# A two-layer encoder trunk on one core: wide products of a weight piece ahead of its narrow ones, and seven-product couples at the front of each pair

## The chip, the core and the metric

The kernel runs on one core of one Trainium2 chip. The metric is the time of one execution on the device in microseconds (us). The kernel before was timed three times; the median counts. One more execution was profiled, and all rows of the trace come from that one.

## What is computed

The reference takes x (256 tokens by 2048 features, float32) through two layers and a last RMSNorm. Cut to what matters:

```python
for layer in range(2):
    hn = rmsnorm(h, norm_mix_g[layer])
    h = h + (mlstm_mixer(hn, ...) if layer == 0 else hgrn_mixer(hn, ...))
    h = h + conv_glu(rmsnorm(h, norm_ffn_g[layer]), w_up[layer], conv_w, conv_b, w_down[layer])
return rmsnorm(h, final_g)

def conv_glu(hn, w_up, conv_w, conv_b, w_down):
    a, v = split(hn @ w_up, 2)          # 2048 -> 2 x 5504
    c = conv_b + sum of three shifted a * conv_w
    return (gelu(c) * v) @ w_down       # 5504 -> 2048
```

Nearly all the work is products with weights, in float32 accuracy, that are read once.

## The kernel before, in words

**Two-part numbers.** TensorE (PE) is given a rounded format, so each operand is sent as a high part and the rest. ScalarE (ACT, L149) casts a raw weight piece of 1024 columns to `wh`, VectorE (DVE, L150) subtracts to get `wl`. An activation tile `xt` holds 256 high and 256 low columns, one for each token. A product with feature-major output ("fm") is two matmuls with a weight block of 128x128 as the stationary operand: `wh` with all 512 columns of `xt` (L338, the wide one), and `wl` with the 256 high columns alone (L342, the narrow one). A 1024-column piece holds four input tiles by two output blocks, thus eight wide and eight narrow matmuls. Line 329 lists them as wide, narrow, wide, narrow, and so on; the tuple `swap` names places where two neighbours change places.

**Stages.** A list of chunks is walked by `stream`: an mLSTM mixer, its output projection, then the feed-forward part of layer 0, the HGRN2 mixer with its projection, and the feed-forward part of layer 1. A feed-forward part has its 43 blocks of 128 hidden features in two parts of 22 and 21 (`FA`, `FB`). Each part is an up pass of as many fm chunks (four pieces each; its results `g`, a high and low half, stay in SBUF), followed by two down pairs. A pair computes two 512-column stretches of the output for both halves of the tokens. In the trace the up passes stand at 400 to 639, 745 to 987, 1690 to 1922 and 2033 to 2266 us, the pairs behind each.

**Pairs.** In a pair, two hidden blocks (a couple, `u`) make a 2x2 block product. The plain way (L297 on) takes eight products, each of three matmuls (high by high, high by low, low by high) of 512 columns: 24 matmuls. Couples listed in `SEVEN` are done in seven products, 21 matmuls, by sums of operand blocks: of the activations (`sx`, made by `token_sums` on DVE at L558 when the second block of the couple has come out of the up pass) and of the weights (`T`). The weight sums of all listed couples but one are made ahead and written to scratch in DRAM (`tscr`), by accumulating DMAs issued on GpSimd (POOL, L611) or on DVE during the up passes (`prepare`, L630), and loaded with the couple; those of couple `FLY` are made on DVE when it is reached (L203). A stored couple loads 1536 raw columns (L137), 1536 columns of sums (L199) and 512 more (L200); a plain couple loads 2048 raw columns. `raw` has three buffers; the `T` tiles share their three (`avc`, L186) with the epilogue of the up chunks (`done_up`, L1178). Pieces are fetched three ahead of their use (`LOOK`).

Four of the products go to banks `mm` of PSUM, and when the last listed couple is through, `mid` (L578) empties them with one copy on ACT, six adds on DVE and two on POOL, by way of a tile `u` with the tag `jk`. The other sums (`pc`) are added at the end of the pair (`done`, L591). In the second pair of a part that ends a layer the last couples are done bank by bank (`tail`, L246), and `bank` of the next norm takes each bank as it is complete: it adds it to the residual `hm`, squares it on ACT (L534, whose output tile has the tag `jk` too), and transposes it (L422) or, at the end of the program, scales it and sends it out (L499 to L530).

**Order.** A scheduler with a timeline of its own sets each engine's order of instructions; `pin` (`keep_in_program_order`) keeps those it is given in the order of the code. Small work is spread between the products by `side.push`, and `tick` moves its clock on.

Of the kernel before, what the change touches and what calls it, by code (L numbers as in the profile page):

```python
# [8 lines left out]
F32 = mybir.dt.float32  # L9
F32R = mybir.dt.float32r  # L10
I32 = mybir.dt.int32
AF = mybir.ActivationFunctionType
# [3 lines left out]
P = 128  # L16
T = 256
# [29 lines left out]
LEAD = 48  # L47
TEMP = 3
GATES = 4 * AH
SEVEN = (1, 2, 3, 4, 5, 6, 7, 8, 9), (1, 2, 3, 4, 5, 6, 7, 8)  # L50
FLY = 5
STORED = 2 * (len(SEVEN[0]) + len(SEVEN[1]) - 2)
BY_TRANSFERS = (9, 27.0), (17, 33.0)
FIRST = 11, 7
# [12 lines left out]
def trunk_kernel(ctx, tc, xT, x_d, fg_d, pp_d, cst_d, w_gate, w_first, w_aq, w_ak, w_av, w_ao, w_aout, w_ao2,  # L67
                 w_bq, w_bv, w_bg, w_bout, w_bo2, w_up, w_d0, w_d1, out, mscr, tscr):
    nc = tc.nc
    act, dve, pool, pe = nc.scalar, nc.vector, nc.gpsimd, nc.tensor  # L70

    keep = ctx.enter_context(tc.tile_pool(name="keep", bufs=1))
# [21 lines left out]
    class Side:  # L94
        def __init__(self):
            self.now, self.jobs, self.behind = 0.0, [], []
# [26 lines left out]
    side, held = Side(), []  # L123


    class Chunk:
        def __init__(self, kind, src, nk, x, done, before=None, swap=(), first=False, paced=False):
            self.swap, self.first, self.paced = swap, first, paced
            self.kind, self.src, self.nk, self.x, self.done, self.before = kind, src, nk, x, done, before
            self.width = {"fm": 256, "tm": 512, "st": 512}[kind]  # L130

    pin = tc.keep_in_program_order
# [90 lines left out]
    def banks():  # L223
        return [psm.tile([P, 512], F32, tag="mm", name="mm") for _ in range(2)]
# [81 lines left out]
    def stream(chunks):  # L306
        pieces = split_weights(chunks)
        ready = []

        def fetch():  # L310
            p = next(pieces, None)
            if p is not None:
                ready.append(p)

        for _ in range(LOOK):
            fetch()
        for ch in chunks:
            if ch.before:
                ch.before()
            if ch.kind == "st":  # L320
                squares_by_seven(ch, fetch, ready)
                continue
            ps = banks()
            k = 0
            while k < ch.nk:
                fetch()
                wh, wl, n = ready.pop(0)
                if ch.kind == "fm":
                    ops = [(kk, f, part) for kk in range(n) for f in range(2) for part in "hl"]
                    for i in ch.swap:  # L330
                        i -= 2 * k
                        if 0 <= i < 2 * n - 1:
                            ops[2 * i + 1:2 * i + 3] = ops[2 * i + 2], ops[2 * i + 1]
                    for kk, f, part in ops:
                        x = ch.x(k + kk)
                        c = kk * ch.width + f * P
                        if part == "h":
                            pe.matmul(ps[f], wh[:, c:c + P], x, start=k + kk == 0, stop=False)  # L338
                            continue
                        if f:  # L340
                            side.tick(0.65)
                        pe.matmul(ps[f][:, 0:T], wl[:, c:c + P], x[:, 0:T], start=False, stop=k + kk == ch.nk - 1)  # L342
                    k += n
                    continue
                for kk in range(n):
                    x = ch.x(k)
                    st, sp = k == 0, k == ch.nk - 1
                    c = slice(kk * 512, (kk + 1) * 512)
                    ops = [(t, i) for t in range(2) for i in range(3)]
                    if ch.first and st:  # L350
                        ops.sort(key=lambda o: (0, 2, 1)[o[1]])
                    for t, i in ops:
                        a, w = ((0, wh), (0, wl), (T, wh))[i]
                        pe.matmul(ps[t], x[:, a + t * P:a + (t + 1) * P], w[:, c], start=st and i == 0, stop=sp and i == 2)  # L354
                    side.tick(1.3)
                    k += 1
            ch.done(ps)
# [21 lines left out]
    class Norm:  # L379
# [46 lines left out]
        def bank(self, ps, i):  # L426
            h = hm[:, i // 2, 512 * (2 + i % 2):512 * (3 + i % 2)]
            dve.tensor_tensor(h, h, ps, ALU.add)
            if i == 3:
                self.add(3)  # L430
                return
            if i == 2:
                self.squares(2)
            for k0 in ((0, 2), (8, 10), (4, 6))[i]:
                self.two(k0, psm.tile([P, 512], F32, tag="mm", name="mm"), pin)
# [34 lines left out]
    class FinalNorm:  # L470
# [5 lines left out]

        def load(self):
            self.g = [keep.tile([P, 512], F32, tag=f"xt{c}", name=f"fg{c}") for c in range(4)]
            for c in range(4):
                pool.dma_start(self.g[c], fg_d[:, c * 512:(c + 1) * 512].broadcast_to([P, 512]))  # L480

        def add(self, c):
            cs = slice(512 * c, 512 * c + 512)
# [15 lines left out]
        def bank(self, ps, i):  # L499
            if i == 0:  # L500
                side.drain()
            t, c = i // 2, 2 + i % 2
            h, total, rc = hm[:, t, 512 * c:512 * c + 512], self.ss[:, t, c:c + 1], self.rc[:, t:t + 1]
            pin(dve.tensor_tensor(h, h, ps, ALU.add))
            if c == 2:
                square(h, total)
                if t:
                    self.store(0)
                pin(dve.scalar_tensor_tensor(rc, total, 1.0 / D, rc, ALU.mult, ALU.add))
                return  # L510
            last = keep.tile([P, 512], F32, tag=f"xt{4 + t}", name="fl")
            pin(dve.scalar_tensor_tensor(last, h, 1.0, h, ALU.mult, ALU.mult, accum_out=total))
            pin(dve.scalar_tensor_tensor(rc, total, 1.0 / D, rc, ALU.mult, ALU.add))
            pool.tensor_tensor(rc, rc, hmx[:, 0:1], ALU.pow)
            v = hm[:, t, 1024:1536]
            pin(dve.tensor_tensor(v, v, self.g[2], ALU.mult))
            if t:
                self.store(1)
# [13 lines left out]
    def square(src, total, pin=lambda ins: ins):  # L532
        jk = ev.tile([P, 512], F32, tag="jk", bufs=1, name="jk")
        pin(act.activation(jk, src, AF.Square, accum_out=total))  # L534
# [630 lines left out]
    def ffn(layer, norm, nxt):  # L1165
# [4 lines left out]
        def begin():  # L1170
            box["mp"] = stack.enter_context(tc.tile_pool(name="ff", bufs=1))
            box["mp"].tile([P, LEAD], F32, name="lead")
            for ch in pairs:
                ch.pool = box["mp"]
            if isinstance(nxt, FinalNorm):
                nxt.begin(box["mp"])
# [28 lines left out]
        for part, (f0, nf) in enumerate(((0, FA), (FA, FB))):  # L1205
            GT, SX, seven = [], {}, SEVEN[part]

            def prep(part=part, nf=nf):
                if part == 0:
                    begin()  # L1210
                n = BY_TRANSFERS[layer][0]
                jobs = todo[n:n + FIRST[layer]] if part == 0 else todo[n + FIRST[layer]:]
                side.push(prepare(box["mp"], jobs, (nf * 10.4 - 26.0) / len(jobs)), True)

            for i in range(nf):
                chunks.append(Chunk("fm", w_up[layer, f0 + i], KT, norm.x, done_up(f0 + i, i, GT, SX, seven),
                                    prep if i == 0 else None,
                                    swap=((2, 12), (2,))[layer] if part and i == 0 else (3,) if f0 + i == 1 else (), paced=True))

            for c0, src in ((0, w_d0[layer][:, f0 * 1024:(f0 + nf) * 1024]), (2, w_d1[layer][:, f0 * 1024:(f0 + nf) * 1024])):  # L1220
                ch = pair(src, nf, c0, lambda k, GT=GT: GT[k], lambda u, SX=SX: SX[u], nxt if part else None, seven)
                ch.waits = []
                for u in seven:
                    if u != FLY:
                        ch.stored[u] = tscr[box["n"]]
                        ch.waits.append(True)
                        todo.append((src[:, 2048 * u:2048 * (u + 1)], tscr[box["n"]], ch.waits))
                        box["n"] += 1
                pairs.append(ch)
                chunks.append(ch)  # L1230
            if part and isinstance(nxt, FinalNorm):
                pairs[-2].before = nxt.load
                pairs[-1].bank, pairs[-1].order = nxt.bank, range(4)
            elif part:
                pairs[-2].later = True
                pairs[-1].bank, pairs[-1].order = nxt.bank, (0, 2, 1, 3)
# [8 lines left out]
    for i in range(90):  # L1245
        o = i % 4 * QUAD
# [6 lines left out]
    c = hgrn(n2, n3)  # L1253
# [108 lines left out]
```

## Time and profile before

| what | value |
|---|---|
| median of 3 runs | 2386.35 us (2380.95 to 2389.92) |
| the profiled execution: its time, its span | 2386.37 us, 2384.4 us |
| PE, DVE, ACT, POOL busy | 99%, 84%, 58%, 12% of the span |
| mean granted clock of PE | 0.998 |
| DMA | 624.32 MB moved, mean 262 GB/s |

The profiled execution lies within 0.02 us of the median, and 1.97 us of its time lie outside the span. Matmuls are pipelined: one is recorded with some 390 ns though the next starts some 230 ns after it, so starts say more than busy times. The waits of an engine are listed by what ended them; "issue" is time in which the profile names nothing.

### The profile page before, as it was taken

What the parts mean: (1) busy time and instruction counts of PE and PEld (TensorE: products, weight loads), DVE (VectorE), ACT (ScalarE), POOL (GpSimd) and SP (SyncE); (2) the same over time, 40 slices, a digit from 0 to 9 for tenths busy, and PEclk for the clock granted to TensorE, in tenths of its full rate; (3) what the DMA queues carried; (4) which work ended last, traced back from release to release, by engine and by line L of the source; (5) the groups of instructions that cost most, each with busy time, mean ns of one, the idle gap of its engine ahead of it and who ended that gap; (6) DMA issues with size and microseconds to landing.
All of it is one profiled execution on the core that took longest, in us unless ns stands there. A gap on an engine that the chain in (4) does not pass through costs nothing.

```text
span 2384.4 us, 38410 instructions
## 1 busy us (share of the span) xinstructions
PE 2361.6 (99%) x14524; PEld 2019.2 (85%) x14524; DVE 1998.9 (84%) x3254; ACT 1393.0 (58%) x2201; POOL 282.4 (12%) x348
## 2 busy tenths in 40 slices
PE   9999999999999999999999999999999999999997
PEld 7888888888888888888888888888888888888876
DVE  7766677988899888898898989889779889888888
ACT  7655455555565555676555555556556576455565
POOL 0110111000000000001333333331010000000000
PEclk9999999999999999999999999999999999999999
DMA  8766878888798888796777777767897788777785
GB/s 299 215 212 232 257 221 274 309 296 289 275 340 305 292 278 280 272 328 219 223 222 232 211 236 222 221 213 235 279 309 274 245 307 325 265 248 243 246 322 203
DMA packets 122986, 624.32 MB, mean 262 GB/s; under 512 B 13856, under 2 KB 14368, under 8 KB 74672
## 3 DMA queue, kind: packets, MB, share of 16 engines
q1 hardware_dynamic: 106128, 590.59, 70.1%
q0 software_dynamic: 16096, 30.48, 8.3%
q8 instruction: 114, 1.87, 0.3%
q10 hardware_dynamic: 576, 0.79, 0.1%
q14 instruction: 72, 0.59, 0.1%
HBM read 584.00 MB, written 92.34 MB: 284 GB/s over the span
## 4 chain that ended last, share of the span: by engine, by line
PE 85%; DVE 5%; DMA 5%; issue 2%; ACT 1%; POOL 1%; SPq 0%; POOLq 0%; DVEq 0%; ACTq 0%
PE mm L338 33%; PE mm L342 17%; PE mm L354 16%; PE pc L236 9%; PE mm L236 7%; DVE wl L150 3%; DMA raw<-in_w_up 1%; DMA T<-tscr 1%; DMA pwh<-in_w_d 1%; DMA raw<-in_w_d 1%; DMA pwl<-in_w_d 1%; PE pn L845 1%; ACT wh L149 1%; PE py L1102 1%; PE pd L1052 0%
## 5 line engine op out<-in xcount | busy, mean ns | idle before, releaser
L338 PE MATMUL mm<-xt,wh 128*128 128x512 f32 x3776 | 1317.9, 394 | 0.0
L150 DVE TENSOR_TENSOR wl<-raw,wh 128x1024 fp32r<-128x1024 f32 (+1 forms) x844 | 1033.7, 1229 | 242.9 <-ACT wh L149 237.0
L149 ACT CAST wh<-raw 128x1024 fp32r<-128x1024 f32 (+1 forms) x844 | 875.2, 1043 | 564.6 <-PE mm L338 295.7
L342 PE MATMUL mm<-xt,wl 128*128 128x256 f32 x3776 | 1051.6, 280 | 1.8 <-issue 1.2
L338 PEld LDWEIGHTS mm<-xt,wh 128*128 128x128 f32 x3776 | 705.8, 187 | 158.9
L342 PEld LDWEIGHTS mm<-xt,wl 128*128 128x128 f32 x3776 | 711.5, 188 | 7.4 <-issue 2.0
L354 PE MATMUL mm<-wh,xt 128*128 128x512 f32 x1024 | 321.7, 393 | 1.8 <-ACT xt L360 1.6
L236 PE MATMUL pc<-wh,g 128*128 128x512 f32 x696 | 237.8, 390 | 0.0
L354 PEld LDWEIGHTS mm<-wh,xt 128*128 128x128 f32 x1024 | 192.1, 188 | 42.2 <-ACT xt L360 2.1
L354 PE MATMUL mm<-wl,xt 128*128 128x512 f32 x512 | 198.7, 392 | 0.0
L236 PE MATMUL mm<-wh,sx 128*128 128x512 f32 x444 | 157.2, 389 | 0.3 <-ACT wh L149 0.3
L149 ACT CAST wh<-T 128x1024 fp32r<-128x1024 f32 (+1 forms) x148 | 122.2, 835 | 55.9 <-DMA T<-tscr 15.6
L236 PEld LDWEIGHTS pc<-wh,g 128*128 128x128 f32 x696 | 130.6, 188 | 27.2
L150 DVE TENSOR_TENSOR wl<-T,wh 128x1024 fp32r<-128x1024 f32 (+1 forms) x148 | 141.5, 967 | 13.1 <-ACT wh L149 12.8
L588 POOL TENSOR_TENSOR hm<-hm,u 128x512 f32<-128x512 f32 x10 | 14.8, 1478 | 1090.4 <-DVE u L587 813.5
L236 PE MATMUL pc<-wl,g 128*128 128x512 f32 x348 | 135.7, 390 | 0.5 <-DVE wl L150 0.5
L354 PEld LDWEIGHTS mm<-wl,xt 128*128 128x128 f32 x512 | 96.6, 189 | 19.1
L1184 ACT COPY avc<-mm 128x256 f32<-128x256 f32 x172 | 64.1, 372 | 69.4 <-PE mm L342 69.4
L236 PEld LDWEIGHTS mm<-wh,sx 128*128 128x128 f32 x444 | 83.2, 188 | 18.0 <-ACT wh L149 0.8
L236 PE MATMUL mm<-wl,sx 128*128 128x512 f32 x222 | 86.6, 390 | 0.6 <-DVE wl L150 0.6
L1189 ACT ACTIVATE avc<-avc,pp 128x256 f32<-128x256 f32 x86 | 51.6, 601 | 57.4 <-DVE avc L1187 57.4
L1185 DVE TENSOR_TENSOR avc<-mm,avc 128x256 f32<-128x256 f32 x172 | 72.2, 420 | 8.6 <-ACT avc L1184 8.4
(248 smaller groups left out, 2444.1 us busy)
## 6 DMA issues: line engine op xcount, KB each, us to landing
raw<-in_w_up SPq DMA_DIRECT2D x172, 1024.0 KB, 5.9
raw<-in_w_bq SPq DMA_DIRECT2D x48, 1024.0 KB, 5.2
raw<-in_w_d SPq DMA_DIRECT2D x60, 768.0 KB, 5.8
T<-tscr SPq DMA_DIRECT2D x60, 768.0 KB, 7.6
tscr<-in_w_d SPq DMA_DIRECT2D x26, 1024.0 KB, 7.5
raw<-in_w_ao SPq DMA_DIRECT2D x24, 1024.0 KB, 6.0
raw<-in_w_d SPq DMA_DIRECT2D x24, 1024.0 KB, 7.0
pwh<-in_w_d SPq DMA_DIRECT2D x36, 512.0 KB, 6.6
```

Source lines behind the costliest of these rows:

```text
L149: pin(act.copy(wh[:, :m], r))
L150: pin(dve.tensor_tensor(wl[:, :m], r, wh[:, :m].bitcast(F32), ALU.subtract))
L236: pin(pe.matmul(ps, a, b, start=id(ps) not in begun, stop=stop and i == 2))
L338: pe.matmul(ps[f], wh[:, c:c + P], x, start=k + kk == 0, stop=False)
L342: pe.matmul(ps[f][:, 0:T], wl[:, c:c + P], x[:, 0:T], start=False, stop=k + kk == ch.nk - 1)
L354: pe.matmul(ps[t], x[:, a + t * P:a + (t + 1) * P], w[:, c], start=st and i == 0, stop=sp and i == 2)
L588: pool.tensor_tensor(part(1, 0), part(1, 0), u, ALU.add)
L845: pe.matmul(pn[:, 0:258], w, v, start=(i == 0), stop=(i == len(parts) - 1))
L1102: pe.matmul(py[:, c], AT[:, s if s == t else 2 + s], V[:, s, j * P:(j + 1) * P], start=(s == 0), stop=(s == 1))
L1184: act.copy(z, p[:, T:2 * T])
L1185: dve.tensor_tensor(z, p[:, 0:T], z, ALU.add)
L1189: act.activation(c, a, AF.Identity, bias=col("conv_b", layer * FT + f), scale=cw[1])
```

## The change

- In every fm piece all eight wide matmuls are listed first, then the eight narrow ones; `swap` is no longer read. In the second part of a feed-forward block the first chunk's matmuls are pinned (`hold`).
- `SEVEN` moves down by one: couples 0 to 8 and 0 to 7 instead of 1 to 9 and 1 to 8. `FLY` is couple 4 instead of 5. Counts stay the same.
- The four loads of `final_g` are spread by `side`, 9 apart, in program order.
- The square of a bank at the end of the program gets a tile of its own (`sq`) in place of `jk`.

```diff
-SEVEN = (1, 2, 3, 4, 5, 6, 7, 8, 9), (1, 2, 3, 4, 5, 6, 7, 8)
-FLY = 5
+SEVEN = (0, 1, 2, 3, 4, 5, 6, 7, 8), (0, 1, 2, 3, 4, 5, 6, 7)
+FLY = 4
...
                     ops = [(kk, f, part) for kk in range(n) for f in range(2) for part in "hl"]
-                    for i in ch.swap:
-                        i -= 2 * k
-                        if 0 <= i < 2 * n - 1:
-                            ops[2 * i + 1:2 * i + 3] = ops[2 * i + 2], ops[2 * i + 1]
+                    ops.sort(key=lambda o: o[2] == "l")
+                    hold = pin if ch.hold and k == 0 else lambda ins: ins
...
-            for c in range(4):
-                pool.dma_start(self.g[c], fg_d[:, c * 512:(c + 1) * 512].broadcast_to([P, 512]))
+            side.push(self.loads(), True)
+
+        def loads(self):
+            for c in range(4):
+                yield 9.0
+                tc.keep_in_program_order(pool.dma_start(self.g[c], fg_d[:, c * 512:(c + 1) * 512].broadcast_to([P, 512])))
...
-                square(h, total)
+                sq = keep.tile([P, 512], F32, tag=f"xt{6 + t}", name="sq")
+                act.activation(sq, h, AF.Square, accum_out=total)
...
-                                    swap=((2, 12), (2,))[layer] if part and i == 0 else (3,) if f0 + i == 1 else (), paced=True))
+                                    swap=(0, 2) if part and i == 0 else (3,) if f0 + i == 1 else (), paced=True,
+                                    hold=part == 1 and i == 0))
```

Lines of code below the first edits move by up to four: the wide and the narrow matmul stand at L336 and L340 in the changed kernel, the pairs' matmuls stay at L236.

On PE, at the end of layer 0's first up pass and the start of the pair behind it, before (`xt` are activations of the up pass, `g` and `sx` those of the pair, `mm` and `pc` the banks):

```order
L338 MATMUL mm<-xt_3905,wh 128x512
L342 MATMUL mm<-xt_3905,wl 128x256
L338 MATMUL mm<-xt_3905,wh 128x512
L342 MATMUL mm<-xt_3905,wl 128x256
L236 MATMUL pc<-wh,g_3982 128x512
L236 MATMUL pc<-wl,g_3982 128x512
L236 MATMUL pc<-wh,g_3982 128x512
L236 MATMUL pc<-wh,g_4088 128x512
```

The same place on PE in the changed kernel:

```order
L336 MATMUL mm<-xt_3907,wh 128x512 x2
L340 MATMUL mm<-xt_3889,wl 128x256 x2
L340 MATMUL mm<-xt_3892,wl 128x256 x2
L340 MATMUL mm<-xt_3904,wl 128x256 x2
L340 MATMUL mm<-xt_3907,wl 128x256 x2
L236 MATMUL mm<-wh,g_3982 128x512
L236 MATMUL mm<-wl,g_3982 128x512
L236 MATMUL mm<-wh,g_3982 128x512
L236 MATMUL pc<-wh,g_3982 128x512
L236 MATMUL pc<-wl,g_3982 128x512
L236 MATMUL pc<-wh,g_3982 128x512
L236 MATMUL mm<-wh,sx 128x512
```

The narrow matmuls now stand in a row, and the seventh matmul of the pair already takes a sum `sx` with weights made from the first `T`; before, that came behind the 24 matmuls of a plain couple and six more.

On the DMA queue of SP at the same place, before (L137 raw weights, L199 and L200 the stored sums):

```order
L137 DMA raw<-in_w_d 128x2048
L137 DMA raw<-in_w_d 128x1536
L200 DMA raw<-tscr 128x512
L199 DMA T<-tscr 128x1536
L137 DMA raw<-in_w_d 128x1536
L200 DMA raw<-tscr 128x512
```

And now:

```order
L137 DMA raw<-in_w_d 128x1536
L200 DMA raw<-tscr 128x512
L137 DMA raw<-in_w_d 128x1536
L200 DMA raw<-tscr 128x512
L199 DMA T<-tscr 128x1536
L137 DMA raw<-in_w_d 128x1536
```

The first stored sums are those of the first couple, and no plain couple's load stands ahead of them. The second `T` waits, in both kernels, for the last `wl` that is made of the first.

On DVE, at the end of the last pair of the program, before (L582 to L587 are `mid`, L504 takes a bank):

```order
L150 TENSOR_TENSOR wl<-raw,wh 128x1024
L582 TENSOR_TENSOR hm<-hm,mm 128x512
L150 TENSOR_TENSOR wl<-raw,wh 128x1024
L584 TENSOR_TENSOR hm<-hm,mm 128x512
L586 TENSOR_TENSOR hm<-hm,mm 128x512
L583 TENSOR_TENSOR u<-u,mm 128x512
L585 TENSOR_TENSOR hm<-hm,u 128x512
L587 TENSOR_TENSOR u<-u,mm 128x512
L504 TENSOR_TENSOR hm<-hm,pc 128x512
```

And now (L585 to L590 are `mid`, L506 takes a bank):

```order
L585 TENSOR_TENSOR hm<-hm,mm 128x512
L587 TENSOR_TENSOR hm<-hm,mm 128x512
L589 TENSOR_TENSOR hm<-hm,mm 128x512
L150 TENSOR_TENSOR wl<-raw,wh 128x1024
L586 TENSOR_TENSOR u<-u,mm 128x512
L150 TENSOR_TENSOR wl<-raw,wh 128x1024 x2
L588 TENSOR_TENSOR hm<-hm,u 128x512
L590 TENSOR_TENSOR u<-u,mm 128x512
L506 TENSOR_TENSOR hm<-hm,pc 128x512
```

Three weight pieces instead of one are now split between the first add of `mid` and the first bank, since one plain couple more follows.

More of the change, by code (lines that the diff above doesn't have):

```diff
@@ L126, in trunk_kernel, with __init__ @@
     class Chunk:
-        def __init__(self, kind, src, nk, x, done, before=None, swap=(), first=False, paced=False):
-            self.swap, self.first, self.paced = swap, first, paced
+        def __init__(self, kind, src, nk, x, done, before=None, swap=(), first=False, paced=False, hold=False):
+            self.swap, self.first, self.paced, self.hold = swap, first, paced, hold
             self.kind, self.src, self.nk, self.x, self.done, self.before = kind, src, nk, x, done, before
@@ L337, in stream @@
                         if part == "h":
-                            pe.matmul(ps[f], wh[:, c:c + P], x, start=k + kk == 0, stop=False)
+                            hold(pe.matmul(ps[f], wh[:, c:c + P], x, start=k + kk == 0, stop=False))
                             continue
@@ L341, in stream @@
                             side.tick(0.65)
-                        pe.matmul(ps[f][:, 0:T], wl[:, c:c + P], x[:, 0:T], start=False, stop=k + kk == ch.nk - 1)
+                        hold(pe.matmul(ps[f][:, 0:T], wl[:, c:c + P], x[:, 0:T], start=False, stop=k + kk == ch.nk - 1))
                     k += n
```

## The prediction

> **What bounds the kernel now.** The page first: which engine is busy, and what the chain that ended last is made of.
>
> ```profile
> span 2384.4 us, 38410 instructions
> PE 2361.6 (99%) x14524; PEld 2019.2 (85%) x14524; DVE 1998.9 (84%) x3254; ACT 1393.0 (58%) x2201; POOL 282.4 (12%) x348
> PE 85%; DVE 5%; DMA 5%; issue 2%; ACT 1%; POOL 1%; SPq 0%; POOLq 0%; DVEq 0%; ACTq 0%
> L338 PE MATMUL mm<-xt,wh 128*128 128x512 f32 x3776 | 1317.9, 394 | 0.0
> ```
>
> PE is the bound nearly everywhere. The change removes no matmul, so it can save only three things: time that PE waits, time that the order of its matmuls costs, and the end of the program, where PE has nothing left. The waits of PE, listed by what ended them:
>
> ```profile
> PE mm L236 <- ACT wh L149: 2.0, 3, 1.5
> ...
> PE mm L422 <- DVE u L587: 1.3, 1, 1.3
> PE mm L342 <- issue: 1.2, 1, 1.2
> ...
> PE mm L236 <- DVE wl L150: 0.6, 1, 0.6
> PE pc L236 <- DVE wl L150: 0.5, 1, 0.5
> PE mm L342 <- DVE wl L150: 0.5, 1, 0.5
> PE pc L236 <- ACT wh L149: 0.5, 1, 0.5
> ```
>
> These seven rows come to 6.6 us, 0.3% of the span. That is the scale of everything here; a measurement of this kernel tells about 0.5% (11.9 us) from no change.
>
> **The wide and narrow matmuls.** The order does cost something already. Here are the same 672 wide matmuls in layer 0's second up pass (745 to 987 us) and in layer 1's (2033 to 2267 us), grouped by line:
>
> ```profile
> L338 PE MATMUL mm<-xt,wh 128*128 128x512 f32 x672 | 237.2, 399 | 0.0
> ...
> L338 PE MATMUL mm<-xt,wh 128*128 128x512 f32 x672 | 232.9, 393 | 0.0
> ```
>
> A wide one is recorded longer than a wide-narrow pair takes, so its busy time covers the pairs: 353.0 ns a pair in one pass and 346.6 in the other, with no wait in either. The kernel holds 3776 pairs; at 346.6 they take 1308.7 us, and 1317.9 is recorded, 9.2 more, of which I put 1.5 down to the overhang of the last wide one at the end of some thirty stretches (an estimate). So 7.7 us are lost to alternating.
>
> What will eight and eight take? Other stages hold runs of one width. PE in order of time, at 91 and at 136 us in the mLSTM mixer:
>
> ```profile
> 91.38 0.40 PE L354 MATMUL mm<-wl,xt 128*128 128x512 f32 x1
> 91.61 0.29 PE L845 MATMUL pn<-Vh,Wh 128*128 128x258 f32 x1
> ...
> 93.77 0.63 PE L354 MATMUL mm<-wh,xt 128*128 128x512 f32 x2
> ...
> 94.92 0.39 PE L354 MATMUL mm<-wl,xt 128*128 128x512 f32 x1
> ...
> 135.78 0.39 PE L354 MATMUL mm<-wl,xt 128*128 128x512 f32 x1
> 136.01 0.40 PE L354 MATMUL mm<-wh,xt 128*128 128x512 f32 x1
> 136.24 0.40 PE L831 MATMUL S<-q,k 128*128 128x256 f32 x2
> ...
> 137.42 0.64 PE L831 MATMUL S<-q,k 128*128 128x256 f32 x4
> ...
> 138.12 0.40 PE L831 MATMUL S<-q,k 128*128 128x256 f32 x2
> ...
> 139.29 0.63 PE L831 MATMUL S<-q,k 128*128 128x256 f32 x4
> ...
> 142.28 0.62 PE L354 MATMUL mm<-wh,xt 128*128 128x512 f32 x2
> ...
> 143.64 0.62 PE L354 MATMUL mm<-wh,xt 128*128 128x512 f32 x2
> ```
>
> From 142.28 to 143.64 stand six wide matmuls alone: 226.7 ns each. A narrow one then has 119.9 of a pair's 346.6, and 256 columns more cost 106.8, 0.42 ns each. Between 91.61 and 93.77 stand 18 of 258 columns: 120 ns each, the same. So neither width is slower in a run of its own; what is open is the passage between them. From 91.38 to 94.92 are six of 512 and the 18 of 258: 6 x 226.7 + 18 x 120.7 = 3.533 us against 3.54, 7 ns for one way in and out. From 135.78 to 142.28 are 22 of 512 and 12 of 256, in four runs: 22 x 226.7 + 12 x 119.9 = 6.43 us against 6.50, 18 ns a run. The 472 pieces (3776 / 8) make one run each: 3.3 us at 7 ns, 8.5 at 18. I take the middle, 12 ns: 5.7 us in place of 7.7, a term of -2.0, with ends of -7.7 (no cost) and +0.8. [...]
>
> The narrow ones also gain cover. The first of a piece now starts 8 x 227 ns after the first wide one instead of 0.23 us after it: 1.6 us later. The longest such wait is marked "issue", but the rows show what it was:
>
> ```profile
> 1537.50 0.40 PE L338 MATMUL mm<-xt,wh 128*128 128x512 f32 x1
> 1539.15 0.39 PE L342 MATMUL mm<-xt,wl 128*128 128x256 f32 x1 [1.25 <-issue]
> ...
> 1537.99 1.23 DVE L150 TENSOR_TENSOR wl<-raw,wh 128x1024 fp32r<-128x1024 f32 x1
> ```
>
> The narrow one at 1539.15 starts when DVE's `wl` ends. Eight wide ones would run till 1539.3, so this wait and the other of L342 go: -1.7 (1.2 + 0.5). If the wide ones should wait for `wh` there, nothing is gained; ACT is at 58%, so I don't expect it. `wh` comes free earlier and `wl` no later, so nothing queues behind. The pinned first chunk only keeps the scheduler from mixing pair and up matmuls: in the terms above.
>
> **The pairs.** All counts stay, so DVE, ACT and DMA do the same work; its place moves.
>
> At the end of a pair, `mid` comes one couple sooner, with a plain couple more behind it. At 1088 us a transpose waited 1.3 us for `mid`'s last read of a bank (the L422 row above). Now 24 more matmuls of 226.7 ns, 5.4 us, lie between: -1.3. The four L236 rows, 3.6 us, are waits for pieces. Some are in a mixer's projection, which the change leaves alone; I take -1.4, with ends of 0 and -3.6, for the same loads and adds stand close together elsewhere.
>
> At the start of a pair behind an up pass, a seven-product couple comes first. The second `T` is loaded once the first has been split. DMA and timing of `T` at 620 to 700 us (the chain, the tile's page), and ACT's and DVE's work from the page:
>
> ```profile
> 642.10 6.18 DMA T<-tscr
> ...
> DMA to landing us min/median/max: 4.4/7.0/8.6
> ...
> L149 ACT CAST wh<-T 128x1024 fp32r<-128x1024 f32 (+1 forms) x148 | 122.2, 835 | 55.9 <-DMA T<-tscr 15.6
> L150 DVE TENSOR_TENSOR wl<-T,wh 128x1024 fp32r<-128x1024 f32 (+1 forms) x148 | 141.5, 967 | 13.1 <-ACT wh L149 12.8
> ```
>
> By the order, the split that frees it now waits for the last chunk's third piece, 2.8 us (8 x 346.6 ns) before the pair (in the last of the four places the second `T` waits for no split), and its first use is the pair's 28th matmul in layer 0's first part (6.1 us in) and the 34th in the other three (7.5 us). That leaves 8.9 or 10.3 us for a split of 0.97, a load of 7.0 and a cast of 0.84, 8.8 us, and their hand-overs. With loads of 8.6 it is 1.5 late once and 0.1 three times. Term +0.4, ends 0 and +1.8.
>
> The spread loads of `final_g` cost POOL nothing: it idles there, and the tiles are read only behind the first pair. Unhidden they would cost `mid`'s POOL adds a few us, off PE's path.
>
> **The end of the program.** DVE, ACT, POOL and PE in order of time:
>
> ```profile
> 2371.78 0.39 PE L236 MATMUL pc<-wh,g 128*128 128x512 f32 x1
> ...
> 2368.43 1.30 POOL L589 TENSOR_TENSOR hm<-hm,u 128x512 f32<-128x512 f32 x1
> ...
> 2369.77 0.63 ACT L534 ACTIVATE jk<-hm 128x512 f32<-128x512 f32 x1 [7.54 <-POOL hm L589]
> ...
> 2370.60 0.68 DVE L504 TENSOR_TENSOR hm<-hm,pc 128x512 f32<-128x512 f32 x1
> ...
> 2375.34 0.68 DVE L504 TENSOR_TENSOR hm<-hm,pc 128x512 f32<-128x512 f32 x1
> ```
>
> The last bank is complete at 2372.2 and taken at 2375.34, because POOL still reads `u` at 2369.7, the square needs its slot, and DVE's adds stand behind the square. With `mid` 5.4 us sooner and `sq` apart, DVE is late by nothing that I can find: -3.1, at least -2.0 if its own queue holds the last bank up by a microsecond.
>
> **The sum**, against the profiled execution (2386.37): -2.0 -1.7 -1.3 -1.4 +0.4 -3.1 = -9.1, so 2377.3 us, 0.4% less than the median of 2386.35.
>
> **The rivals.**
> - *Clean runs.* The time of a matmul follows from its columns alone and a passage costs nothing, so all passes run at 346.6 a pair: the first term is -7.7 and the sum -14.8, 2371.6. For it: 232.9 is reached in an order that alternates every time. Against: the 18 ns above. [...]
> - *Waits that only move.* The pairs' pieces and the narrow matmuls wait as long elsewhere, since DVE works 84% of the span, and the runs cost what alternating did: only L422 and the end are saved, -4.4, 2382.0.
> - *No lead for the loads* (slower). DMA, from the page, and the span of layer 0's first pairs by engine:
>
> ```profile
> raw<-in_w_d SPq DMA_DIRECT2D x60, 768.0 KB, 5.8
> T<-tscr SPq DMA_DIRECT2D x60, 768.0 KB, 7.6
> ...
> 640.00:745.00 105.00, 104.24 (x456) 84.90 (x456) 95.88 (x108) 73.54 (x87) 3.54 (x2) 1.00 0.87 319
> ```
>
> A stored couple moves 768 + 768 + 256 KB, 1.84 MB, at 319 GB/s 5.8 us, but its 21 matmuls take 4.8. A plain couple moves 1.05 MB (3.3 us) in 5.4 us, and before one stood ahead of the listed ones: 2.1 us of lead, at four pairs 8.4 us. If that lead is what kept PE fed, it is paid at every one of them: 8.4 us if the lead alone is lost, 32 (4 pairs x 8 stored couples x 1.0) if the buffers carry nothing. Before, they carried most of it without a wait, so I take a price of 12: 2389.3. It turns slower than before once a pair's start costs over 2.3 us (9.1 / 4). Against it: three `raw` and the first `T` stand loaded in the up pass.
>
> **How the numbers follow.** Forecast 0.45, clean runs 0.22, waits that move 0.2, no lead 0.13. The forecast's ends: 2386.37 - 7.7 - 1.7 - 1.3 - 3.6 - 3.1 is 2369.0, and 2386.37 + 0.8 - 1.7 - 1.3 + 1.8 - 2.0 is 2384.0. The last rival's time is 2389.3, and single runs before lie up to 5.4 us from their median. 2368 to 2390 takes these in; it leaves out the dear half of the last rival and the best of the clean runs. Faster by over 0.5% means under 2374.4: most of the clean runs and a little of the forecast, 0.25. Slower means over 2398.3, a price of 21 in the last rival: 0.05. The rest, 0.70, is no change.
>
> **What would show it.** Right: the runs of eight at 227 and 120 ns with 5 to 8 us over in all; no wait of the narrow matmuls for `wl`; no wait of L422 for `mid`; the last bank taken within 0.5 us of PE's last matmul. Wrong: narrow runs over 125 ns each, which would cost 472 x 8 x 5 ns = 19 us; waits for `T` or `raw` of over 2 us at the start of pairs behind up passes; the last bank still taken 3 us late.

## The result: 0.4% slower, and the profile after

The changed kernel takes 2395.71 us (median of 13 runs, 2389.06 to 2398.60). Beside it on the same chip the kernel before takes 2384.59 (13 runs). The ratio over all runs is 1.0036, with a 95% interval of 1.0025 to 1.0047: 8.6 us more (the two medians lie 11.1 us apart). That is no change by the bound of 0.5%, but the forecast was 2377.3 with a range to 2390, and the sign is wrong.

The page of the changed kernel, the same lines as before:

```profile
span 2394.4 us, 38507 instructions
PE 2368.0 (99%) x14524; PEld 2030.8 (85%) x14524; DVE 1995.9 (83%) x3254; ACT 1389.8 (58%) x2201; POOL 279.3 (12%) x348
...
q8 instruction: 114, 1.87, 0.3%
```

PE's waits by what ended them:

```profile
PE pd L1055 <- issue: 8.2, 4, 3.0
PE mm L336 <- DVE avc L1188: 2.5, 1, 2.5
PE mm L236 <- ACT wh L149: 2.2, 4, 0.8
...
PE pc L236 <- ACT wh L149: 1.0, 2, 0.6
...
PE mm L420 <- DVE xt L359: 0.3, 1, 0.3
```

The waits that I wanted gone are gone: no narrow matmul waits for `wl`, and no transpose waits for `mid`. Two new ones stand on top. L1055 is the small matmuls of a HGRN head, and "issue" means that the profile names no one.

Where the 10.1 us of span went can be read from PE's starts. A matmul that follows its neighbour freely starts 226.7 ns later at 512 columns and 120 at 256, the two paces in the prediction; the other widths are put on the line through these two, 13.3 ns and 0.4167 ns a column. What the gaps have over that is summed here by stage, with the time from the last matmul's start to the end of the span. The line fits these two widths alone; the smaller matmuls are the same in both kernels, so it is the differences that count. The stages' times are those of the kernel before:

| stage | before | after | difference |
|---|---|---|---|
| start and mLSTM, to 342 us | 12.0 | 9.4 | -2.6 |
| its projection, to 402 us | 3.4 | 4.6 | +1.2 |
| the four up passes | 6.0 | 11.4 | +5.4 |
| HGRN, 1094 to 1606 us | 21.0 | 31.2 | +10.2 |
| pairs and the other projection | 9.1 | 7.3 | -1.8 |
| behind the last matmul | 12.6 | 10.3 | -2.3 |

The pairs and the end gain roughly as forecast. The gain at the start can't be put down to the change: PE's first wait for `xt` is 1.6 us in the kernel before and absent here, but it is 0.3 us in `e10_sq` below too, where the program's start is that of the kernel before. HGRN, which the change touches only by the order inside a piece, loses most. The same 500 us of it by engine (PE first), before:

```profile
1100.00:1600.00 500.00, 497.82 (x4584) 427.58 (x4583) 438.76 (x900) 273.02 (x526) 178.22 (x224) 1.00 0.73 222
```

and after:

```profile
1100.00:1600.00 500.00, 490.75 (x4408) 422.83 (x4407) 426.58 (x878) 266.63 (x510) 169.07 (x223) 0.99 0.73 219
```

PE stands still for 9.2 us of them, against 2.2 before, and does less in the same window. Here is one of the four places, head 2, in order of time:

```profile
1207.82 0.56 PE L1055 MATMUL pa<-kq 128*32 128x64 f32 x32
...
1208.36 0.82 PE L1055 MATMUL pd<-kq 128*32 128x32 f32 x69
...
1208.77 2.35 DVE L150 TENSOR_TENSOR wl<-raw,wh 128x1024 fp32r<-128x1024 f32 x2
...
1211.04 0.49 DVE L1047 COPY kq<-QK 128x256 f32<-128x256 f32 x2
1211.07 0.27 PE L1055 MATMUL pd<-kq 128*32 128x32 f32 x9 [1.90 <-issue]
```

PE stops in the middle of the head and goes on at 1211.07. My first reading was that the last `kq`, a gather on DVE, is late behind two `wl`. This was the theory of the first four runs, and it is wrong; one sign is already here: PE goes on 0.03 us after that copy starts, not after it ends.

The other new wait lies in layer 0's first up pass:

```profile
414.64 1.11 PE L340 MATMUL mm<-xt,wl 128*128 128x256 f32 x8
415.48 0.69 DVE L652 TENSOR_TENSOR pwh<-pwh 128x512 f32<-128x512 f32 x1 [8.19 <-DMA pwh<-in_w_d]
...
416.09 1.22 DVE L150 TENSOR_TENSOR wl<-raw,wh 128x1024 fp32r<-128x1024 f32 x1
417.22 0.68 DVE L652 TENSOR_TENSOR pwh<-pwh 128x512 f32<-128x512 f32 x1
417.83 0.75 DVE L1188 TENSOR_TENSOR avc<-mm,avc 128x256 f32<-128x256 f32 x2
...
418.30 0.68 PE L336 MATMUL mm<-xt,wh 128*128 128x512 f32 x1 [2.55 <-DVE avc L1188]
```

DVE stood 8.2 us before an addition of `prepare` whose data had not landed; behind it in the queue stood the epilogue that frees PE's bank.

### The profile page after: what moved, and what is told of

Same layout as the page of the kernel before. It is cut to its first block, busy times and chain, and to the rows that moved or that the text cites. A ratio compares the mean times of both kernels' runs of the same rounds, so it can differ in the third digit from the quotient of the medians.

```text
span 2394.4 us, 38507 instructions
## 1 busy us (share of the span) xinstructions
PE 2368.0 (99%) x14524; PEld 2030.8 (85%) x14524; DVE 1995.9 (83%) x3254; ACT 1389.8 (58%) x2201; POOL 279.3 (12%) x348
## 3 DMA queue, kind: packets, MB, share of 16 engines
q8 instruction: 114, 1.87, 0.3%
## 4 chain that ended last, share of the span: by engine, by line
PE 90%; DVE 5%; DMA 2%; issue 1%; ACT 1%; POOL 0%; SPq 0%; POOLq 0%; DVEq 0%; ACTq 0%
PE mm L336 35%; PE mm L340 18%; PE mm L352 16%; PE pc L236 10%; PE mm L236 7%; DVE wl L150 3%; DMA T<-tscr 1%; PE pn L848 1%; ACT wh L149 1%; DMA pwh<-in_w_d 1%; PE py L1105 1%; PE pd L1055 1%; PE pa L1055 0%; DMA raw<-in_w_ao 0%; PE pz L420 0%
## 5 line engine op out<-in xcount | busy, mean ns | idle before, releaser
L336 PE MATMUL mm<-xt,wh 128*128 128x512 f32 x3776 | 952.9, 393 | 2.5 <-DVE avc L1188 2.5
L336 PEld LDWEIGHTS mm<-xt,wh 128*128 128x128 f32 x3776 | 679.9, 189 | 124.2 <-DVE avc L1188 2.8
L340 PEld LDWEIGHTS mm<-xt,wl 128*128 128x128 f32 x3776 | 516.7, 190 | 37.1
L340 PE MATMUL mm<-xt,wl 128*128 128x256 f32 x3776 | 532.9, 283 | 0.0
L236 PE MATMUL pc<-wh,g 128*128 128x512 f32 x696 | 237.9, 390 | 0.1
L236 PE MATMUL mm<-wh,sx 128*128 128x512 f32 x444 | 155.3, 390 | 2.2 <-ACT wh L149 2.2
L236 PEld LDWEIGHTS pc<-wh,g 128*128 128x128 f32 x696 | 130.6, 188 | 27.8 <-ACT wh L149 0.7
L150 DVE TENSOR_TENSOR wl<-T,wh 128x1024 fp32r<-128x1024 f32 (+1 forms) x148 | 140.1, 964 | 13.8 <-ACT wh L149 11.2
L591 POOL TENSOR_TENSOR hm<-hm,u 128x512 f32<-128x512 f32 x10 | 21.2, 2118 | 1080.7 <-DVE u L590 1033.1
L236 PE MATMUL pc<-wl,g 128*128 128x512 f32 x348 | 135.4, 389 | 0.0
L236 PEld LDWEIGHTS mm<-wh,sx 128*128 128x128 f32 x444 | 82.9, 188 | 21.1 <-ACT wh L149 4.2
L236 PE MATMUL mm<-wl,sx 128*128 128x512 f32 x222 | 86.4, 389 | 0.0
L1073 POOL TENSOR_TENSOR G<-G 128x384 f32<-128x384 f32 (+2 forms) x96 | 76.6, 798 | 4.6
L236 PEld LDWEIGHTS pc<-wl,g 128*128 128x128 f32 x348 | 65.3, 188 | 13.6 <-DVE wl L150 0.2
L1047 DVE COPY kq<-QK 128x256 f32<-128x256 f32 x224 | 71.1, 342 | 0.2
```

The costliest lines, as they stand in the source:

```text
L150: pin(dve.tensor_tensor(wl[:, :m], r, wh[:, :m].bitcast(F32), ALU.subtract))
L236: pin(pe.matmul(ps, a, b, start=id(ps) not in begun, stop=stop and i == 2))
L336: hold(pe.matmul(ps[f], wh[:, c:c + P], x, start=k + kk == 0, stop=False))
L340: hold(pe.matmul(ps[f][:, 0:T], wl[:, c:c + P], x[:, 0:T], start=False, stop=k + kk == ch.nk - 1))
L591: pool.tensor_tensor(part(1, 0), part(1, 0), u, ALU.add)
L1047: dve.tensor_copy(m[:, j].rearrange("k (m p j) -> k m p j", p=2, j=h), blocks(z, h, 0, T))
```

## The experiments

All ratios are to the kernel before on the same chip; its time was 2382.3 to 2385.1 us beside them.

**One part at a time.** `e1_pairs` is the changed kernel with the old order inside a piece:

```diff
-                    ops.sort(key=lambda o: o[2] == "l")
-                    hold = pin if ch.hold and k == 0 else lambda ins: ins
+                    for i in ch.swap:
...
+                    hold = lambda ins: ins
```

> The changed kernel with the old order inside a piece (wide and narrow in turn, the old places of swap, nothing pinned in an up chunk); the pairs, the spread loads and the square's own tile stay changed. Theory (the order of the products lost the time, the pairs and the end gained): 2379, 5 us under the kernel before, with the last bank taken at once and no transpose waiting for mid. Rival 1 (each passage between wide and narrow costs 22 ns in place of 12, 10 us in all): the same 2379. Rival 2 (the pairs' loads lost their lead, and that is the loss): slower than before, 2390 or more, with waits for T and raw at the starts of pairs.

Measured: 2380.59 us, ratio 0.9985 (0.9974 to 0.9997). The pairs, the loads and the end gain 3.6 us. The rival on the pairs' lead falls: nothing is lost at the starts of pairs.

`e2_order` is the kernel before with `ops.sort` and `hold` alone.

> The kernel before with nothing but the new order inside a piece and the pinned first up chunk of second parts. Theory (side work and DVE's queue are shifted by the new order, so the HGRN heads' last small matmuls wait): 2400, 15 us over the kernel before, about 10 of them between 1100 and 1600 us, in a few stalls of 1.5 to 3 us behind two wl in a row on DVE. Rival 1 (passages): 2394 to 2400 too, but spread evenly, 22 ns at each of 472 pieces. Rival 2 (pairs): 2381, the runs gain and the pairs are the old ones.

Measured: 2397.70, ratio 1.0058 (1.0045 to 1.0071), 13.8 us more, with four HGRN stalls (7.7 us) and the one at 415 us. The loss belongs to the order inside a piece.

`e3_ticks` moves the ticks of side work, which spread the small work between the products:

```diff
-                    for kk, f, part in ops:
+                    for o, (kk, f, part) in enumerate(ops):
+                        if o in (3, 6, 9, 15):
+                            side.tick(0.65)
...
-                        if f:
-                            side.tick(0.65)
```

> The changed kernel, with the four ticks of side work in a piece set ahead of its matmuls 4, 7, 10 and 16, about 0.7 us apart, in place of ahead of four of the last eight. Theory: side work is spread as before, the stalls of the HGRN heads go for the most part: 2387. Rival 1 (passages): 2396 as the changed kernel. Rival 2 (pairs): 2396. If the stalls stay, it is the scheduler's own placing by the order of the matmuls and not the ticks.

Measured: 2389.41, ratio 1.0024 (1.0011 to 1.0037). Half of what was expected. The stall at 415 us is gone, so it came from the ticks, which the new order had put together at the back of a piece: DVE still waits 5.9 us for such data there, but where PE doesn't wait for DVE. In HGRN three of the four stalls stay (6.3 us), so the ticks are not their cause.

`e4_up` keeps eight and eight in the up passes alone:

```diff
-                    ops.sort(key=lambda o: o[2] == "l")
+                    if ch.paced:
+                        ops.sort(key=lambda o: o[2] == "l")
```

> The changed kernel with eight and eight in the up passes alone (344 pieces), the old turns in the two mixers (128 pieces). Theory: the mixers' stages go back to what they took before, 9.6 us in HGRN and 1.9 in the first one: 2384, with the stall near 415 us still there. Rival 1 (passages, 22 ns at each piece): only 128 x 22 ns = 2.8 us come back: 2393. Rival 2 (pairs): 2396.

Measured: 2396.78, ratio 1.0056 (1.0042 to 1.0069). The theory of the side work and the rival of the passages both miss: HGRN's own products stand in the old order again, and it still has three stalls. The number is that of the rival on the pairs, but `e1_pairs` had ruled that one out, and the stalls are not in the pairs. Head 2 in this run:

```profile
1210.97 0.90 PE L1056 MATMUL pd<-kq 128*32 128x32 f32 x78
...
1212.17 2.35 DVE L150 TENSOR_TENSOR wl<-raw,wh 128x1024 fp32r<-128x1024 f32 x2
1214.44 0.49 DVE L1048 COPY kq<-QK 128x256 f32<-128x256 f32 x2
...
1215.05 0.80 PE L353 MATMUL mm<-wh,xt 128*128 128x512 f32 x1 [3.18 <-issue]
```

The head is through, and the stall comes behind it, ahead of a matmul whose weights ACT had cast by 1211.15, almost 4 us before. Data is not what PE waits for. So the first theory fell, and I looked at what else goes to PE: its code.

**The code.** The page has a DMA queue of kind "instruction", q8: 114 packets, 1.87 MB, 16 KB each (a second one, q14, moves 0.58 MB in all). In the built program PE has 29,317 instructions: the 14,524 weight loads and 14,524 matmuls of the page, and 269 others, nearly all of them waits that stand by themselves. 29,317 / 114 is 257, so I took a packet for a block of about 256 instructions. A head is 256 instructions in 1.25 us, where 256 of the other stages, 128 matmuls of 226.7 ns, take 29 us. In head 2 of the changed kernel the packet moves while PE runs the head; DMA between 1208.70 and 1208.80 us:

```profile
q8 instruction: 1, 0.02, 58.3%
```

Between 1201 and 1208.70 us there is none. PE goes on 2.3 us after this packet started. I then counted PE's instructions in the built programs up to each place where the profile marks "issue" and two matmuls start over 0.9 us apart. In all 14 profiles (of both kernels and of the twelve runs of this section) there are 31; each is ahead of instruction 193 or 194 of 256, counted from the program's first. In each of them PE goes on 2.2 to 3.0 us after the last packet of q8 started, and that packet started 0.6 to 4.3 us after PE had begun the block that it was running. The four of the changed kernel's heads are ahead of instructions 13761, 16066, 18369 and 20674, 2304 (9 x 256) apart to within one. I read it so: PE stops where a block ends, because the next one is not there. That a block ends at 193 or 194 is read from these stalls; the count alone doesn't say it. The block before had been used up in 1.2 to 4.2 us, since most of a head lay in it or, at the program's start, the warm-up matmuls. New theory: the change shifts PE's stream so that a block's end stands among the last 20 instructions of heads 2, 6, 10 and 14.

What shifts it is in the program too: before a wide matmul there are 6 separate wait instructions in the kernel before, and 170 in the changed one. The first wide matmul of the second bank stood behind a narrow one, whose wait for DVE's `wl` covered DVE's release of the bank. Now both banks are begun with a wide one, each needs a wait for ACT (or for PE) and one for DVE, and one of the two becomes an instruction: in the built programs of both kernels no matmul carries more than one wait.

`e5_phase` shifts the stream by 32, with 8 more of the warm-up matmuls that the program starts with (4 instructions each: for 90 of them the trace has 180 weight loads and 180 matmuls), and leaves the order of all engines as it is from 350 us on:

```diff
-    for i in range(90):
+    for i in range(98):
         o = i % 4 * QUAD
         pe.matmul(idle[o:o + QUAD, 0:53], ones[:, 0:QUAD], ones[:, 0:53], start=True, stop=True)
```

> The changed kernel with 98 in place of 90 warm-up matmuls at its start, 32 instructions more in PE's stream; from 350 us on every engine's order is the same as in the changed kernel. Theory (PE's code arrives in blocks of 256 instructions; heads 2, 6, 10 and 14 of HGRN, 256 instructions in 1.2 us, stand so that PE is through with one block before the next has been loaded): the heads then stand 32 further on, the four stalls marked issue and the halved clock behind two of them go, 11 us: 2385, a start 0.3 us later counted. Rival (their last gather is late on DVE behind two wl): nothing changes in HGRN: 2396.

Measured: 2393.82, ratio 1.0032 (1.0021 to 1.0043). The mechanism is borne out, the time is not: 2385 was expected. The four stalls are gone, and three new ones stand behind heads 3, 7 and 11: there the shift had put a block's end among the first dozen instructions, so that the head fell to the next block and used most of it up. Behind head 3:

```profile
1228.31 0.50 PE L1055 MATMUL pd<-kq 128*32 128x32 f32 x36
...
1228.73 0.62 PE L340 MATMUL mm<-xt,wl 128*128 128x256 f32 x3
...
1231.61 0.28 PE L340 MATMUL mm<-xt,wl 128*128 128x256 f32 x1 [2.26 <-issue]
```

`e6_badphase` is the reverse, on the good kernel: `e1_pairs` with `range(113)`, so that its heads stand where those of the changed kernel stood.

> The run with the old order inside a piece and the new pairs (2380.6), with 113 in place of 90 warm-up matmuls: 92 instructions more in PE's stream, the order otherwise the same on every engine, so that heads 2, 6, 10 and 14 stand where they stood in the changed kernel. Theory (code blocks): stalls of 2 to 3 us at three or four of these heads, and the start up to 1 us later: 2389 to 2393. Rival (DVE's order, or the wide products first): no stalls, 2381 to 2382.

Measured: 2402.91, ratio 1.0069 (1.0050 to 1.0087), against 0.9985: 20 us lost by 23 warm-up matmuls at the program's start, more than expected. The profiled execution is 26.8 us longer than that of `e1_pairs`; the gaps of PE's starts in HGRN show 12.0 us of stalls, and 7.5 us of matmuls at half their pace behind them (the execution's mean granted clock is 0.994, against 0.998 in `e1_pairs`), and 4 us lie in layer 1's first up pass, which ran at 353 ns a pair in place of 347. The kernel's work and its order on every engine are those of `e1_pairs`, but for one small matmul of the first mixer that stands a place earlier. Its largest wait, a row that `e1_pairs` doesn't have, and head 2:

```profile
PE pd L1058 <- issue: 10.5, 3, 4.7
```

```profile
1207.97 0.83 PE L1058 MATMUL pd<-kq 128*32 128x32 f32 x70
...
1209.18 2.35 DVE L150 TENSOR_TENSOR wl<-raw,wh 128x1024 fp32r<-128x1024 f32 x2
1211.45 0.49 DVE L1050 COPY kq<-QK 128x256 f32<-128x256 f32 x2
1211.80 0.34 PE L1058 MATMUL pd<-kq 128*32 128x32 f32 x8 [2.99 <-issue]
```

These are the rows of the changed kernel's head 2, in the old order of products. That settles the cause of the HGRN stalls.

`e7_ticks_phase` is `e3_ticks` with `range(98)`.

> The changed kernel with the ticks spread as in the third run and with 98 warm-up matmuls. Theory (code blocks and ticks are the two losses that matter): no stall at 415 us and none in the heads: 2389.4 less 7 us, 2382. Rival: 2389.

Measured: 2390.37, ratio 1.0023 (1.0014 to 1.0032): no gain, for the reason of `e5_phase`; the stalls stand behind heads 3, 7 and 11.

`e9_clear` is `e3_ticks` with `range(108)`.

> The changed kernel with the ticks spread as in the third run and with 108 warm-up matmuls, 72 instructions more in PE's stream in place of 32: by the count no head of HGRN is now followed by a block's end within 35 instructions of its own end. Theory (code blocks): no stall marked issue of over 1 us in HGRN at all, neither in heads 2, 6, 10, 14 nor behind 3, 7, 11; 2389.4 less 7 to 8 us, and 0.5 for the later start: 2382. Rival (the stalls belong to the order of wide and narrow and only change places): a stall of 2 us at some three or four other heads: 2389.

Measured: 2388.97, ratio 1.0022 (1.0011 to 1.0034). Without a stall 2382 was expected. One is left, of 3.3 us in head 11, at instruction 194 again: I had looked only at ends of blocks behind a head, and here one block ends 27 instructions ahead of the head and the next 27 ahead of its end. The time is no lower than that of `e3_ticks`, though its profile holds 3.3 us of stalls in HGRN against 6.3: what a profile's stalls come to is not what the median shows.

`e12_all_clear` is `e3_ticks` with `range(110)`.

> The changed kernel with the ticks spread and with 110 warm-up matmuls, 8 instructions more in PE's stream than in the ninth run, where head 11 alone still stood still for 3.3 us; by the count every head of HGRN now keeps clear of a block's end. Theory (code blocks): no stall marked issue of over 1 us between 1100 and 1600 us; the excess of that stage over its matmuls' own pace falls to that of the kernel before (20 us), and the time to 2389.0 - 4.5 = 2384.5, level with the kernel before: what the pairs and the end gain, the runs of eight and eight cost elsewhere. Rival (the stalls wander with the new order of the products): a stall of 2 us or more at some head, 2388.

Measured: 2385.79, ratio 1.0014 (1.0005 to 1.0023), 1.3 us over what was expected. In HGRN the stalls of 2 to 3 us are gone; two of 1.1 and 1.2 us are left, some 3 us behind heads 0 and 8, at instruction 194, and one of 2.2 us came at the program's start, at instruction 193, among the warm-up's blocks. HGRN's excess falls from 31.2 to 24.0. By ticks and a shift, with no change to the products' order, 5 of the 8.6 us are won back, 2.9 of them with the ticks alone (`e3_ticks`).

**The rest.** `e10_sq` is the kernel before with the square's own tile:

```diff
-                square(h, total)
+                sq = keep.tile([P, 512], F32, tag=f"xt{6 + t}", name="sq")
+                act.activation(sq, h, AF.Square, accum_out=total)
```

> The kernel before with the square's own tile at the end and nothing else. If that edit ends the late last bank: 2 to 2.5 us less between PE's last matmul and the span's end (12.6 before, 10.3 in the changed kernel): 2382.5. If the earlier mid of the pairs does it: 12.6 as before, 2384.6.

Measured: 2383.08, ratio 0.9997 (0.9986 to 1.0008). From PE's last matmul to the end it takes 11.7 us, against 12.6 before and 10.1 in `e1_pairs`. But `e2_order`, whose end is that of the kernel before, takes 13.4, so 0.9 is no more than two profiles of one end differ by: a share of the tile is not shown. All runs that have both edits take 10.1 to 10.4, so the two together do gain, and the tile alone does not bring it. The time can't tell it either.

`e8_second_up` is `e1_pairs` with the new order in one pass:

```diff
+                    if ch.block:
+                        ops.sort(key=lambda o: o[2] == "l")
...
+                                    hold=part == 1 and i == 0, block=part == 1 and layer == 0))
```

> The run with the old order inside a piece and the new pairs, with eight and eight in layer 0's second up pass alone (84 pieces), where the old order ran at 353 ns a pair. Theory (a run of eight and eight costs 19 ns a piece over 346.6, in any pass): 349.2 ns a pair there, 84 x 8 x 3.8 = 2.6 us less: 2378. Rival (the order inside a piece moves the code blocks and the side work again): 2381 or more.

Measured: 2377.96, ratio 0.9972 (0.9962 to 0.9982), as expected. It beats both kernels, by 6.7 us the one before.

`e11_second_up_clear` is the same with `range(93)`.

> The run with eight and eight in layer 0's second up pass alone (2377.96), with three warm-up matmuls more, 12 instructions, so that head 13, which stood still for 1.2 us in it, is clear of the block's end. Theory (code blocks): that stall goes, 2377.0 with the start 0.1 us later. Rival: 2378 and the stall stays, or another comes.

Measured: 2376.03, ratio 0.9972 (0.9962 to 0.9983). The stall of head 13 is gone from the profile; in time it is level with `e8_second_up`.

## Why the prediction was wrong, step by step

- **The order of wide and narrow, -2.0.** This is the step that failed, twice. First, its price: the pieces of layer 0's second up pass, in order of time, PE alone:

```profile
900.58 2.00 PE L336 MATMUL mm<-xt,wh 128*128 128x512 f32 x8
902.42 1.12 PE L340 MATMUL mm<-xt,wl 128*128 128x256 f32 x8
903.37 2.00 PE L336 MATMUL mm<-xt,wh 128*128 128x512 f32 x8
905.21 1.11 PE L340 MATMUL mm<-xt,wl 128*128 128x256 f32 x8
906.16 2.00 PE L336 MATMUL mm<-xt,wh 128*128 128x512 f32 x8
```

  A piece starts every 2.79 us; the mean is 349.1 ns a pair in all four passes. Before they ran at 346.9, 353.3, 346.9 and 346.7 (mean of the gaps between starts, stalls left out). The passage costs 19 ns a piece, not 12: behind a narrow run the first five wide ones take 233, 236, 228, 232 and 231 ns in place of 226.7, and the first narrow one 113 in place of 120. Over the 344 pieces of the up passes that is 2752 x 2.5 ns = 6.9 us over 346.6, against 5.0 before: a loss of 1.9, where the whole term was a gain. The rival of clean runs falls with it: a passage does cost something, and inside a run the last three wide ones take 226.7 ns each and the last six narrow ones 120, as in the prediction.
- Second, "so nothing queues behind". I costed the order by PE's pace alone. It also set the ticks (415 us: a stall of 2.7 and 1.7 of slow matmuls behind it) and PE's count of instructions (HGRN: 9.0 us of stalls and 3.0 of slow matmuls). These 16 us, of the profiled execution, are most of the miss of 18.4. That the change still counts as none is luck: the sum had no such terms.
- **The cover for `wl`, -1.7.** The 0.5 us row is gone as forecast. The 1.2 us row, at 1539.15 us, was misread: it stands at the same place of a block as the others, so I read it as a wait for code: PE went on ahead of instruction 194 of a block, 2.45 us after a packet of q8 had started. The rows spoke against `wl`: PE started at 1539.15, and `wl` ended at 1537.99 + 1.23 = 1539.22, after it. "Issue" did mean that no one was named.
- **The pairs' end, -1.3.** Right: 0.3 us of another wait is left.
- **The pieces in the pairs, -1.4.** Wrong, and the rival "waits that only move" right: 3.6 us before, 3.2 in the changed kernel and 3.4 in `e1_pairs`.
- **The pairs' start, +0.4.** No more than that: in `e1_pairs` no wait at a pair's start is over 0.5 us, where the third rival needs 2 us. That rival's time, 2389.3, came nearest, by a mechanism that did not happen.
- **The end, -3.1.** It is -2.3, for the two edits together. The last bank was taken 3.56 us after the start of the last matmul, and is now taken 1.09 after it, 0.7 after its end:

```profile
2384.13 0.39 PE L236 MATMUL pc<-wh,g 128*128 128x512 f32 x1
...
2385.22 0.68 DVE L506 TENSOR_TENSOR hm<-hm,pc 128x512 f32<-128x512 f32 x1
```

What stays open: why the next block comes so late. In head 2 of the changed kernel the running block began 17 instructions ahead of the head, at 1206.37 us, its packet started at 1208.75, and PE went on at 1211.07, 4.7 after the block began; in head 10 of `e6_badphase` it took over 6, though the packet of head 2 in the changed kernel took 0.93 us (58.3% of 16 engines in 0.1 us). The place alone does not make a stall: in `e3_ticks` head 2 stands at the same place, but the packet had started at 1200.27, 3 us before the running block, and PE did not stop. What sets the packet's start was not found. And how the stalls fall in executions that weren't profiled isn't known.

## What to carry to other kernels

An order of instructions has more prices than its pace: it moves what is tied to it (ticks, waits that covered other waits), and by the count of instructions where PE's code blocks end. Where a stage issues a block's worth of tiny matmuls in about a microsecond (here 256 instructions in 1.25 us), compare that count with each stall that is marked "issue" before believing in a data wait; a few harmless instructions far ahead test it. And a row that names no releaser is not to be given one by nearness: compare start and end first.

## What the runs showed of the hardware

- **PE's code came in blocks, and this stopped PE.** 31 stalls, of 1.2 to 4.9 us from start to start, all at one place of a 256-instruction block, moved by 8 and by 23 warm-up matmuls (`e5_phase`, `e6_badphase`). PE goes on 2.2 to 3.0 us after the block's packet started. Of the 114 packets of the changed kernel, 16 KB each, four came with such a stall, all at heads.
- **The granted clock fell to half behind three of the changed kernel's stalls.** Behind the stall of head 6, by engine, with the granted clock third from the right:

```profile
1334.00:1337.00 3.00, 1.01 (x73) 0.84 (x60) 3.00 (x6) 1.38 (x5) 0.00 (x0) 0.94 0.81 246
1337.00:1340.00 3.00, 3.00 (x8) 2.35 (x9) 3.00 (x15) 0.00 (x0) 0.00 (x0) 0.50 0.98 333
1340.00:1344.00 4.00, 4.00 (x19) 3.28 (x18) 2.79 (x7) 3.40 (x8) 0.00 (x0) 0.99 0.88 352
```

  PE does 8 matmuls in 3 us at a granted clock of 0.50 and goes on at 0.99; it had been idle for 2.0 us (1334.56 to 1336.55). The clock is 0.50 for the next 3 us behind the stalls at 415 us (2.55 us idle) and of head 10 (2.99 us) too. Behind those of heads 2 (1.90 us) and 14 (1.38 us) it stays at 1.00. What sets it is not shown.
- **The old order has two paces.** A pass of alternating matmuls runs at 346.7 or at 353 ns a pair, and with the same order of instructions up to there layer 1's first pass ran at 346.9 in the kernel before and at 353.0 in `e10_sq`. Eight and eight ran at 349.1 to 349.4 in every pass, stretches at half the clock left out. What sets the pace was not found.
